# Pool's subtractions in pieces, a modulation sum spread ahead of the last feed-forward group, turned buffer places, and filler products in a router

## The chip, the cores and the metric

The kernel runs on one core of one Trainium2 chip. The metric is the device time of one execution in microseconds (us). Before the change three runs gave 2020.33 to 2025.81 us with a median of 2025.24 us. The engines of the core run side by side, each working through its own list of instructions in order: PE (matrix products; PEld is its weight load), DVE (VectorE), ACT (ScalarE), POOL (GpSimd) and SP, which here only starts the DMA loads of weights.

## The reference

The model is a backbone of two layers over 256 latent tokens and 256 context tokens of width 1024. Layer 0 runs grouped-query attention and gated linear attention side by side, then a dense SwiGLU with 3584 hidden features. Layer 1 is a neighbourhood attention and a top-2-of-8 mixture of experts with the same hidden width per expert. Each layer is modulated by six vectors of 1024 that come from the conditioning by one product with w_mod (adaln):

```python
for i in range(DEPTH):
    sh1, sc1, gt1, sh2, sc2, gt2 = _adaln(c, w_mod[i], b_mod[i])       # silu(c) @ w_mod + b_mod
    cmod = _adaln(c_ctx, w_mod[i], b_mod[i])
    h_lat = _modulate(_rmsnorm(x, g_norm1[i]), sh1, sc1)
    ...                                                               # mixer of layer i, y_lat, y_ctx
    x = x + gt1 * y_lat
    x = x + gt2 * ffn(_modulate(_rmsnorm(x, g_norm2[i]), sh2, sc2))    # SwiGLU in layer 0, experts in layer 1
    if need_ctx:
        ctx = ctx + cmod[2] * y_ctx
        ctx = ctx + cmod[5] * ffn(_modulate(_rmsnorm(ctx, g_norm2[i]), cmod[3], cmod[4]))
return _rmsnorm(x, g_final)

def _moe(h, w_router, wg, wu, wd):
    top_v, top_i = lax.top_k((h @ w_router).astype(jnp.float32), TOP_K)
    ...                                                               # softmax of the two, sum over experts
```

## The kernel before

Products of layer 0, of the neighbourhood attention's projections and of the dense feed-forward are done in three parts, because a weight and its input are each split into a high and a low half (hi and lo). For a weight of 1 MB (128 partitions x 2048 columns) `load_split` (L181 to L203) does that: SP loads it into a `raw` place, ACT casts it to `whi` (L201), and DVE subtracts the two into `wlo` (L202). Four of the weights, and the second pair of some projections, have POOL do this subtraction instead (`low = nc.gpsimd`). `raw`, `whi` and `wlo` each turn over a few places; a counter `state["n"]` decides which place the next `whi` and `wlo` get (three of each in the feed-forward). A place is free when its last reader is done.

A scheduler orders the instructions of each engine by priority in the order of the program; weight loads and their splits are moved ahead (`PREP`).

The parts that the change touches stand in the program in this order.

- **Layer 0's projections and output** (180 to 346 us): POOL subtracts `wlo8` (read by `pt_rb`) and `wlo12` (read by `po_gqa`).
- **The feed-forward of layer 0** (346 to 832 us): a loop over 7 groups of 512 hidden features. A group forms the products `pf_fg` and `pf_fu` for four blocks j, ACT and DVE form `sg` and `fT`, and then eight banks `fd{g}_{t}_{half}` of 12 products each go through DVE into the residual `xr` (`rtmp_ff`, then `xr`; L726, L727).
- **The modulation of layer 1**, three parts (1,0), (1,1), (1,2) of 2048 columns, is a sum on DVE (`adaln_sums`, L254 to L291) that is cut in 10 steps each: a load, eight products with a row block of `w_mod` (`acc`, L278 for the first and L280 for the others; (1,0) has three DVE instructions in each step instead of one), and an end with four products on PE and four transposes (`mod_ps`, `m_sb`, `modT_ps`, `mT`). `tick()` releases one step. The feed-forward loop calls it in two of a group's four blocks, and in all four blocks of the last group, so 16 of 30 steps; `tick(24)` (L971) releases the rest after the loop.
- **The norm after it** (`n3`): ACT squares, DVE `ms_n`, POOL `rs_n`, DVE `xc`, PE transposes `tf_n3`, and then per block of features ACT and DVE form `f_hi`, `tfraw` and `f_lo` (L369 to L372). Two streams of 256 tokens, context first. `mT` of part (1,0) and the parts after it go into this modulation. Then the projections `pt_vc` start, whose first weights are `whi`/`wlo` 56 and 57.
- **The neighbourhood attention's output** (to 1077 us): POOL subtracts the last such weight, read by `po_c`. POOL also adds a constant to `bias` (L1046).
- **The router** (1075 to 1094 us): for two blocks t of 128 tokens, `route_turn` transposes `xr` into `xT` (`rt`), `route_logits` squares and forms the norm and the logits (`lt_ps`, `lg_ps`, `lg`), `route_top` picks two experts (`sel`) and ranks tokens (`rk_ps`). Then PE gathers tokens (`gx`), and the first expert's products `pg_e` begin. From there to 2000 us the experts' products run.

Of the kernel before, what the change touches and what calls it, by code (L numbers as in the profile page):

```python
# [89 lines left out]
def kernel(ctx, tc, x, c, ctx_in, c_ctx, w_mod, b_mod, g_norm1, g_norm2, w_in_ab, g_q, g_k,  # L90
# [1034 lines left out]

    def route_turn(t):
        xt = xr[2 + t]
        for f4 in range(2):
            ps = bankB(f"rt_{t}_{f4}")
            for f in range(4):  # L1130
                o = (4 * f4 + f) * P
                nc.tensor.transpose(out=ps[:, f * P:(f + 1) * P], in_=xt[:, o:o + P], identity=ident)
            ins = (nc.scalar.copy if f4 or t == 0 else nc.vector.tensor_copy)(xT[:, t, 4 * f4:4 * f4 + 4, :],
                                                              ps.rearrange("p (f n) -> p f n", n=P))

        critical["turn"] = (ins.ins,)

    def route_logits(t):

        ssq = small.tile([P, 2], F32, tag="ssq2", name=f"ssq_n4_{t}")  # L1140
        ms = small.tile([P, 2], F32, tag="ms2", name=f"ms_n4_{t}")
        for h in range(2):
            hs = slice(h * 512, h * 512 + 512)
            nc.scalar.activation(xs_hi[t][:, hs], xr[2 + t][:, hs], AF.Square, accum_out=ssq[:, h:h + 1])
# [374 lines left out]
```

## Time and profile before

| what | value |
|---|---|
| median of 3 runs | 2025.24 us |
| the profiled execution's own time | 2025.02 us |
| its span (first to last instruction) | 2023.0 us |
| PE busy | 1933.7 us, 96% of the span |
| DVE busy | 750.6 us, 37% |
| ACT busy | 448.9 us, 22% |
| POOL busy | 148.9 us, 7% |
| DMA, moved | 493.32 MB |

The profiled execution lies 0.22 us below the median of the runs; 2.02 us of it are outside the span. In the pages below a time ahead of a row is counted from the start of the span. `PEclk` is the share of TensorE's full clock that was granted.

### The profile page before, as it was taken

The page shows a single profiled execution, that of the slowest core. Times are in us where ns is not written, and L with a number is a line of the kernel's source. Part 1 is how long each engine was busy: PE and PEld are TensorE (multiplying, and loading weights), DVE is VectorE, ACT ScalarE, POOL GpSimd, SP SyncE. Part 2 cuts the span into 40 slices and gives each one's busy share as a digit, 9 for nine tenths or more (in the row PEclk, how much of TensorE's full clock was granted, in tenths as well). Part 3 has the DMA queues.
Part 4 walks back from the last instruction along what each step waited for, and adds up shares of the span by engine and source line. Part 5 has one row for each costly group of instructions (what it writes and reads, how often), then busy time and mean ns, then how long its engine had stood idle before and what let it go on. Part 6 is the DMA issues. An engine that isn't in the chain of part 4 may idle for free.

```text
span 2023.0 us, 37020 instructions
## 1 busy us (share of the span) xinstructions
PE 1933.7 (96%) x16599; PEld 1182.6 (58%) x16599; DVE 750.6 (37%) x1185; ACT 448.9 (22%) x732; POOL 148.9 (7%) x145
## 2 busy tenths in 40 slices
PE   5999988999999999699998999999999999999996
PEld 3666666888888788467765354545444444544433
DVE  3246587656545555826773001111010101111022
ACT  4232255421222122235543001010100001010001
POOL 1102000000000000143211000000000100001010
PEclk8999999999999999799998999999999999999998
DMA  8624210433333334463336999999999999999991
GB/s 329 231 85 167 81 46 28 166 127 117 125 115 106 133 125 168 168 177 99 107 112 257 395 409 372 379 409 389 383 382 396 402 381 362 383 409 387 403 396 47
DMA packets 118901, 493.32 MB, mean 244 GB/s; under 512 B 10656, under 2 KB 50912, under 8 KB 98256
## 3 DMA queue, kind: packets, MB, share of 16 engines
q1 hardware_dynamic: 114096, 481.04, 62.4%
q0 software_dynamic: 3216, 7.03, 1.5%
q8 instruction: 132, 2.16, 0.4%
q10 hardware_dynamic: 1424, 2.81, 0.4%
q14 instruction: 33, 0.27, 0.0%
HBM read 486.13 MB, written 4.72 MB: 243 GB/s over the span
## 4 chain that ended last, share of the span: by engine, by line
PE 92%; DVE 4%; issue 1%; DMA 1%; ACT 1%; POOL 1%; ACTq 0%; SPq 0%; POOLq 0%; DVEq 0%
PE pu_e L1280 15%; PE pg_e L1280 14%; PE py_e L1280 14%; PE pf_fg L473 3%; PE pf_fg L471 3%; PE pf_fg L472 3%; PE fd L208 3%; PE pf_fu L473 3%; PE pf_fu L472 3%; PE pf_fu L471 3%; PE fd L206 3%; PE fd L207 3%; PE sc_e L1355 1%; PE mod_ps L245 1%; PE gx L1268 1%
## 5 line engine op out<-in xcount | busy, mean ns | idle before, releaser
L1280 PE MATMUL pu_e<-raw,X_all 128*32 128x448 f32 x3072 | 306.1, 540 | 0.0
L1280 PE MATMUL py_e<-raw,eT_e 128*32 128x256 f32 x5376 | 296.5, 379 | 0.0
L1280 PE MATMUL pg_e<-raw,X_all 128*32 128x448 f32 x3024 | 291.4, 539 | 0.0
L1280 PEld LDWEIGHTS py_e<-raw,eT_e 128*32 128x32 f32 x5376 | 190.5, 110 | 105.0 <-issue 5.4
L1280 PEld LDWEIGHTS pg_e<-raw,X_all 128*32 128x32 f32 x3024 | 100.0, 110 | 181.2 <-issue 175.5
L1280 PEld LDWEIGHTS pu_e<-raw,X_all 128*32 128x32 f32 x3072 | 98.5, 110 | 182.4 <-issue 178.4
L202 DVE TENSOR_TENSOR wlo<-raw,whi 128x2048 fp32r<-128x2048 f32 (+1 forms) x67 | 149.3, 2237 | 130.4 <-ACT whi L201 130.3
L201 ACT CAST whi<-raw 128x2048 fp32r<-128x2048 f32 (+1 forms) x73 | 134.9, 1859 | 257.8 <-PE fd L208 115.2
L1317 DVE TENSOR_TENSOR m_sb<-m_sb,pu_e 128x448 f32<-128x448 f32 x48 | 27.8, 604 | 393.6 <-PE pu_e L1280 393.6
L1313 ACT ACTIVATE m_sb<-pg_e 128x448 f32<-128x448 f32 x48 | 26.1, 544 | 512.8 <-PE pg_e L1280 512.8
L1358 POOL TENSOR_TENSOR xr<-xr,ytmp_e 128x512 f32<-128x512 f32 x28 | 35.2, 1280 | 822.5 <-DVE ytmp_e L1357 822.5
L473 PE MATMUL pf_fg<-f_hi,wlo 128*128 128x512 f32 (+1 forms) x240 | 92.5, 385 | 1.3 <-DVE ms_n L338 1.3
L472 PE MATMUL pf_fg<-f_lo,whi 128*128 128x512 f32 (+1 forms) x240 | 92.1, 384 | 0.0
L471 PE MATMUL pf_fg<-f_hi,whi 128*128 128x512 f32 (+1 forms) x240 | 92.0, 383 | 0.0
L471 PE MATMUL pf_fu<-f_hi,whi 128*128 128x512 f32 (+1 forms) x240 | 92.0, 383 | 0.0
L472 PE MATMUL pf_fu<-f_lo,whi 128*128 128x512 f32 (+1 forms) x240 | 91.6, 382 | 0.0
L473 PE MATMUL pf_fu<-f_hi,wlo 128*128 128x512 f32 (+1 forms) x240 | 91.2, 380 | 0.0
L208 PE MATMUL fd<-whi,fT 128*128 128x512 f32 x224 | 88.8, 396 | 0.0
L206 PE MATMUL fd<-whi,fT 128*128 128x512 f32 x224 | 88.5, 395 | 0.0
L207 PE MATMUL fd<-wlo,fT 128*128 128x512 f32 x224 | 88.3, 394 | 0.0
L1357 DVE SCALAR_TENSOR_TENSOR ytmp_e<-sc_e,comb,gate 128x512 f32<-128x512 f32 x32 | 23.6, 749 | 165.4 <-PE sc_e L1355 160.5
L1348 ACT COPY yF<-py_e 32x256 f32<-32x256 f32 x48 | 17.4, 362 | 265.9 <-PE py_e L1280 257.6
(373 smaller groups left out, 2707.8 us busy)
## 6 DMA issues: line engine op xcount, KB each, us to landing
raw<-in_w_moe_up_dram SPq DMA_DIRECT2D x128, 896.0 KB, 6.5
raw<-in_w_moe_down_dram SPq DMA_DIRECT2D x112, 1024.0 KB, 8.4
raw<-in_w_moe_gate_dram SPq DMA_DIRECT2D x126, 896.0 KB, 7.2
raw<-in_w_mod_dram SPq DMA_DIRECT2D x48, 1024.0 KB, 4.8
raw<-in_w_ff_gate_dram SPq DMA_DIRECT2D x14, 1024.0 KB, 4.9
raw<-in_w_ff_up_dram SPq DMA_DIRECT2D x14, 1024.0 KB, 4.9
raw<-in_w_ff_down_dram SPq DMA_DIRECT2D x14, 1024.0 KB, 4.9
raw<-in_w_in_c_dram SPq DMA_DIRECT2D x12, 1024.0 KB, 5.2
```

The source lines that it names most:

```text
L201: nc.scalar.copy(hi[:, c], raw[:, c])
L202: low.tensor_tensor(lo[:, c], raw[:, c], hi[:, c].bitcast(F32), op=ALU.subtract)
L206: nc.tensor.matmul(ps, ah, bh, start=start, stop=False)
L207: nc.tensor.matmul(ps, ah, bl, start=False, stop=False)
L208: nc.tensor.matmul(ps, al, bh, start=False, stop=stop)
L471: nc.tensor.matmul(ps, wh[:, k, ws], hh[:, k, ts], start=(k == 0), stop=False)
L472: nc.tensor.matmul(ps, wh[:, k, ws], hl[:, k, ts], start=False, stop=False)
L473: nc.tensor.matmul(ps, wl[:, k, ws], hh[:, k, ts], start=False, stop=(k == KT - 1))
L1280: nc.tensor.matmul(out[32 * q:32 * q + 32], lhsT, rhs[:, q], start=start, stop=stop, skip_group_check=True)
L1313: nc.scalar.activation(g, ps[s][:, 0:QW], AF.Silu)
L1317: nc.vector.tensor_tensor(gs[s], gs[s], ps[s][:, 0:QW], op=ALU.mult)
L1358: (nc.vector if self.last else nc.gpsimd).tensor_tensor(xr[2 + t][:, hs], xr[2 + t][:, hs], tmp, op=ALU.add)
```

## The change

Four things are done. First, where POOL subtracts in `load_split`, the subtraction is cut into instructions of 256 columns, so eight for a whole weight, and the addition to `bias` is cut in three. Second, `tick()` is called in all four blocks of each odd group and in two of an even group, so 20 steps of the modulation are released inside the feed-forward instead of 16, and `tick(24)` has 10 left. Third, the counter `state["n"]` is raised by one ahead of the feed-forward and once more ahead of the neighbourhood attention, so that each later weight takes the next place. The raised counter also changes the numbers in the names: `whi56` before is `whi58` after. Fourth, in the router the squares come ahead of the copies, POOL's `r_n4` with them, and 14 products `warm` that nobody reads are put between the steps on PE.

```diff
                 nc.scalar.copy(hi[:, c], raw[:, c])
-                low.tensor_tensor(lo[:, c], raw[:, c], hi[:, c].bitcast(F32), op=ALU.subtract)
+                if low is nc.vector:
+                    low.tensor_tensor(lo[:, c], raw[:, c], hi[:, c].bitcast(F32), op=ALU.subtract)
+                else:
+                    a, b, l = (w[:, c].rearrange("p k n -> p (k n)") for w in (raw, hi, lo))
+                    n = a.shape[-1]
+                    for o in range(0, n, 256):
+                        low.tensor_tensor(l[:, o:o + 256], a[:, o:o + 256], b[:, o:o + 256].bitcast(F32),
+                                          op=ALU.subtract)
...
+    state["n"] += 1
     queue_adaln((1, 0), (1, 1), (1, 2))
...
-                if j % 2 or g == NG - 1:
+                if j % 2 or g % 2:
                     tick()
...
+    state["n"] += 1
     for half in range(2):
         def ev_v(t, ps, half=half):
...
-        nc.gpsimd.tensor_tensor(bv, bv, cc(C_WIN, 64).unsqueeze(1).to_broadcast([P, 12, 64]), op=ALU.add)
+        for o in range(0, 12, 4):
+            nc.gpsimd.tensor_tensor(bv[:, o:o + 4], bv[:, o:o + 4],
+                                    cc(C_WIN, 64).unsqueeze(1).to_broadcast([P, 4, 64]), op=ALU.add)
...
+    warm_ps = bankA("warm")
+    def warm(n, after):
+        with tc.issue_after(after):
+            for _ in range(n):
+                nc.tensor.matmul(warm_ps[:, 0:256], ident, gate2[:, 0:256], start=True, stop=True)
+
     def route_turn(t):
...
+            sq = nc.scalar.activation(xs_hi[t][:, hs], xt[:, hs], AF.Square, accum_out=ssq[:, f4:f4 + 1]).ins
...
+            if t == 1:
+                warm(2 if f4 else 5, turned)
+            with tc.issue_after(sq):
+                (nc.scalar.copy if f4 or t == 0 else nc.vector.tensor_copy)(xT[:, t, 4 * f4:4 * f4 + 4, :],
+                                                                            ps.rearrange("p (f n) -> p f n", n=P))
...
+        if t == 1:
+            warm(3, mm.ins)
...
+        if t == 0:
+            warm(4, critical["rank"])
```

DVE at the end of the feed-forward, before: `fd6_2` and `fd6_3` are the last banks of the last group, `acc1_2` is the sum of part (1,2), `tfraw_n3` and `f_lo` the norm's stream of context tokens.

```order
L352 TENSOR_SCALAR xc1_5748<-xr2_1594,rs_n3_1_0_5753 128x1024
L727 TENSOR_TENSOR xr3_1595<-xr3_1595,rtmp_ff6_3_0_5600 128x512
L726 TENSOR_TENSOR rtmp_ff6_3_1_5616<-fd6_3_1_5603,gate0_0_5_2737 128x512
L727 TENSOR_TENSOR xr3_1595<-xr3_1595,rtmp_ff6_3_1_5616 128x512
L293 TENSOR_TENSOR m_sb1_1588<-mod_ps1_1_5626,m_sb1_1588 128x512
L278 TENSOR_SCALAR acc1_2_5639<-raw96_5640,cT_76 128x2048
L300 COPY mT1_96<-modT_ps1_1_5632 128x16 x2
L280 SCALAR_TENSOR_TENSOR acc1_2_5639<-raw97_5642,cT_76,acc1_2_5639 128x2048
L371 TENSOR_SCALAR tfraw_n3_0_0_5702<-tf_n3_0_0_5696,A3_1_5679,mT1_96 128x256
L280 SCALAR_TENSOR_TENSOR acc1_2_5639<-raw98_5645,cT_76,acc1_2_5639 128x2048
L372 TENSOR_TENSOR f_lo_2427<-tfraw_n3_0_0_5702,f_hi_828 128x256
L280 SCALAR_TENSOR_TENSOR acc1_2_5639<-raw99_5648,cT_76,acc1_2_5639 128x2048
```

The eight steps of `acc1_2` stand behind the last bank's residual, between the steps of the norm. After:

```order
L966 TENSOR_TENSOR sg6_3_5495<-sg6_3_5495,pf_fu6_1_1_5393 128x512
L301 TENSOR_TENSOR m_sb1_1595<-mod_ps1_1_5500,m_sb1_1595 128x512
L968 TENSOR_TENSOR fT1_6_5254<-sg6_3_5495,fT0_6_5253 128x512
L286 TENSOR_SCALAR acc1_2_5653<-raw96_5654,cT_76 128x2048
L308 COPY mT1_96<-modT_ps1_1_5506 128x16 x2
L288 SCALAR_TENSOR_TENSOR acc1_2_5653<-raw97_5656,cT_76,acc1_2_5653 128x2048
L734 TENSOR_TENSOR rtmp_ff6_0_0_5538<-fd6_0_0_5525,gate0_1_5_2744 128x512
L288 SCALAR_TENSOR_TENSOR acc1_2_5653<-raw98_5659,cT_76,acc1_2_5653 128x2048
L735 TENSOR_TENSOR xr0_1599<-xr0_1599,rtmp_ff6_0_0_5538 128x512
L288 SCALAR_TENSOR_TENSOR acc1_2_5653<-raw99_5662,cT_76,acc1_2_5653 128x2048
L734 TENSOR_TENSOR rtmp_ff6_0_1_5554<-fd6_0_1_5541,gate0_1_5_2744 128x512
L288 SCALAR_TENSOR_TENSOR acc1_2_5653<-raw100_5665,cT_76,acc1_2_5653 128x2048
```

The same sum now starts ahead of the first bank's residual (`fd6_0_0`) and stands between the residuals of the first four banks; its eighth step comes just before the residual of `fd6_1_1`, and the norm's `tfraw` and `f_lo` have none of it between them.

POOL in the same stretch, before: `rs_n3` are the norm's scales of four blocks of tokens, `rb_s` loads of a table, `wlo57` a subtraction for `pt_vc`.

```order
L340 TENSOR_TENSOR rs_n3_0_0_5686<-ms_n3_0_0_5684,mhalf_74 128x1
L340 TENSOR_TENSOR rs_n3_0_1_5693<-ms_n3_0_1_5691,mhalf_74 128x1
L340 TENSOR_TENSOR rs_n3_1_0_5753<-ms_n3_1_0_5751,mhalf_74 128x1
L340 TENSOR_TENSOR rs_n3_1_1_5760<-ms_n3_1_1_5758,mhalf_74 128x1
L987 MEMSET rb_s_5836 112x128
L989 DMA rb_s_5836<-in_rpb_c_dram 7x31 x3
L202 TENSOR_TENSOR wlo57_5878<-raw105_5875,whi57_5877 128x2048
L989 DMA rb_s_5836<-in_rpb_c_dram 7x31 x13
L990 DMA rb_d_5817<-rb_s_5836 7168x1x128
```

After:

```order
L997 MEMSET rb_s_5850 112x128
L999 DMA rb_s_5850<-in_rpb_c_dram 7x31 x6
L348 TENSOR_TENSOR rs_n3_0_0_5700<-ms_n3_0_0_5698,mhalf_74 128x1
L999 DMA rb_s_5850<-in_rpb_c_dram 7x31 x4
L348 TENSOR_TENSOR rs_n3_0_1_5707<-ms_n3_0_1_5705,mhalf_74 128x1
L999 DMA rb_s_5850<-in_rpb_c_dram 7x31 x6
L209 TENSOR_TENSOR wlo59_5892<-raw105_5889,whi59_5891 128x256 x8
L348 TENSOR_TENSOR rs_n3_1_0_5767<-ms_n3_1_0_5765,mhalf_74 128x1
L1000 DMA rb_d_5831<-rb_s_5850 7168x1x128
L348 TENSOR_TENSOR rs_n3_1_1_5774<-ms_n3_1_1_5772,mhalf_74 128x1
```

The subtraction (now `wlo59`, eight instructions) stands between the second and the third of the norm's scales, and the table's loads ahead of it; before, it stood behind all four.

PE in the router, before: `rt`, `lt_ps`, `lg_ps` and `rk_ps` are the router's steps, the last figure of a name the block t.

```order
L1152 MATMUL lt_ps0_7649<-xT_7616,wrA_6117 32x128 x8
L1132 MATMUL rt_1_1_7635<-ident_69,xr3_1595 128x128 x4
L1157 MATMUL lg_ps0_7660<-cst_71,lt0_7658 128x8
L1152 MATMUL lt_ps1_7673<-xT_7616,wrA_6117 32x128 x8
L1157 MATMUL lg_ps1_7684<-cst_71,lt1_7682 128x8
L1179 MATMUL rk_ps0_7705<-sel_7609,cst_71 128x8
L1178 MATMUL rk_ps1_7727<-sel_7609,cst_71 128x8
```

After:

```order
L1145 MATMUL warm_7675<-gate1_0_5_6129,ident_69 128x256 x5
L1158 MATMUL rt_1_1_7711<-ident_69,xr3_1602 128x128 x4
L1145 MATMUL warm_7675<-gate1_0_5_6129,ident_69 128x256 x2
L1175 MATMUL lt_ps0_7723<-xT_7674,wrA_6138 32x128 x8
L1180 MATMUL lg_ps0_7734<-cst_71,lt0_7732 128x8
L1175 MATMUL lt_ps1_7739<-xT_7674,wrA_6138 32x128 x8
L1180 MATMUL lg_ps1_7750<-cst_71,lt1_7748 128x8
L1145 MATMUL warm_7675<-gate1_0_5_6129,ident_69 128x256 x3
L1204 MATMUL rk_ps0_7774<-sel_7667,cst_71 128x8
L1145 MATMUL warm_7675<-gate1_0_5_6129,ident_69 128x256 x4
L1203 MATMUL rk_ps1_7800<-sel_7667,cst_71 128x8
L1204 MATMUL rk_ps1_7800<-sel_7667,cst_71 128x8
```

`lt_ps0` now stands behind the last transposes `rt_1_1`, and fillers stand ahead of them, behind them, ahead of `rk_ps0` and between the two rank products.

## Rows read from the trace of the kernel before

**Rows 1.** Windows: PE, PEld, DVE, ACT, POOL busy (instructions), PEclk, DMA share, GB/s.
```profile
400.00:450.00 50.00, 50.00 (x216) 40.14 (x215) 30.26 (x29) 11.71 (x11) 0.00 (x0) 1.00 0.35 121
1150.00:1200.00 50.00, 50.00 (x680) 24.89 (x676) 3.38 (x6) 0.36 (x1) 0.00 (x0) 1.00 1.01 410
```
**Rows 2.** SP's queue: line waited for, us in total, times, longest.
```profile
SPq L168 <- PE pu_e L1280: 263.6, 121, 5.9
```
**Rows 3.** Timeline of PE, end of the feed-forward: start, duration, operation, [idle before <-releaser].
```profile
831.57 0.40 PE L208 MATMUL fd<-whi,fT 128*128 128x512 f32 x1
...
839.20 1.12 PE L362 MATMUL tf_n<-ident,xc 128*128 128x128 f32 x4 [4.34 <-ACT tfraw_n L369]
847.11 0.47 PE L362 MATMUL tf_n<-ident,xc 128*128 128x128 f32 x1 [6.79 <-ACT tfraw_n L369]
853.60 1.94 PE L286 MATMUL mod_ps<-acc,one_of 128*32 128x512 f32 x8 [6.02 <-DVE acc L280]
...
864.15 0.66 PE L362 MATMUL tf_n<-ident,xc 128*128 128x128 f32 x4 [3.19 <-ACT tfraw_n L369]
...
875.29 0.40 PE L208 MATMUL pt_vc<-whi,f_lo 128*128 128x512 f32 x1
```
**Rows 4.** Timeline of DVE in the same stretch.
```profile
833.94 1.28 DVE L278 TENSOR_SCALAR acc<-raw,cT 128x2048 f32<-128x2048 f32 x1
...
858.28 4.31 DVE L372 TENSOR_TENSOR f_lo<-tfraw_n,f_hi 128x256 fp32r<-128x256 f32 x1
```
**Rows 5.** Windows in the same stretch.
```profile
801.00:831.00 30.00, 30.00 (x131) 24.23 (x130) 15.51 (x23) 6.47 (x9) 1.65 (x3) 1.00 0.10 36
855.00:860.00 5.00, 4.90 (x22) 3.56 (x19) 5.00 (x4) 2.78 (x3) 4.08 (x5) 0.64 0.32 74
```
**Rows 6.** Timeline of POOL in the same stretch.
```profile
857.72 4.58 POOL L202 TENSOR_TENSOR wlo<-raw,whi 128x2048 fp32r<-128x2048 f32 x1
```
**Rows 7.** POOL's groups: count, busy us, mean ns, idle before.
```profile
L202 POOL TENSOR_TENSOR wlo<-raw,whi 128x2048 fp32r<-128x2048 f32 x6 | 27.9, 4648 | 90.0 <-ACT whi L201 90.0
...
L1046 POOL TENSOR_TENSOR bias<-bias,cst 128x768 f32<-128x768 f32 x8 | 15.3, 1922 | 16.8 <-DMA bias<-rb_d 16.8
...
L1198 POOL TENSOR_TENSOR xs_lo<-scaled,xs_hi 128x512 fp32r<-128x512 f32 x4 | 5.0, 1282 | 13.8 <-ACT scaled L1197 13.8
```
**Rows 8.** Timeline of DVE beside POOL's subtractions.
```profile
275.66 4.51 DVE L727 TENSOR_TENSOR xr<-xr,rtmp_gla 128x512 f32<-128x512 f32 x1
...
1041.04 0.68 DVE L727 TENSOR_TENSOR xr<-xr,rtmp_c 128x512 f32<-128x512 f32 x1
...
1045.64 5.05 DVE L727 TENSOR_TENSOR xr<-xr,rtmp_c 128x512 f32<-128x512 f32 x1
```
**Rows 9.** Timeline of PE behind these.
```profile
187.60 0.79 PE L207 MATMUL pt_rb<-wlo,h_hi 128*128 128x512 f32 x1 [3.73 <-POOL wlo L202]
...
280.83 0.37 PE L798 MATMUL qT_ps<-ident_r,qhl 128*128 128x128 f32 x2 [4.19 <-DVE kT L788]
...
1051.68 0.65 PE L851 MATMUL o_c<-PT_c,vc 128*64 128x256 f32 x2 [2.20 <-DVE oC L854]
```
**Rows 10.** Timeline of PE where the feed-forward starts.
```profile
349.49 0.55 PE L362 MATMUL tf_n<-ident,xf 128*128 128x128 f32 x3 [2.99 <-DVE xf L352]
```
**Rows 11.** DVE's groups: the modulation's sums.
```profile
L280 DVE SCALAR_TENSOR_TENSOR acc<-raw,cT,acc 128x2048 f32<-128x2048 f32 x21 | 49.3, 2348 | 24.5 <-DMA raw<-in_w_mod_dram 24.4
...
L280 DVE SCALAR_TENSOR_TENSOR m_sb<-raw,cT,m_sb 128x1024 f32<-128x1024 f32 x7 | 9.0, 1279 | 0.0
```
**Rows 12.** Timeline of PE in the router.
```profile
1085.64 7.94 PE L1268 MATMUL gx<-m_sb,xr 128*128 128x192 f32 x32
1093.51 0.96 PE L1280 MATMUL pg_e<-first,X_all 128*32 128x448 f32 x8
```
**Rows 13.** Windows of `gx` alone: PE busy (instructions), PEclk.
```profile
1086.00:1088.00 2.00, 2.00 (x7) 2.00 (x7) 0.00 (x0) 0.50 0.99 412
1091.50:1093.40 1.90, 1.90 (x13) 1.79 (x11) 1.48 (x4) 1.00 1.03 426
```

More of the change, by code (lines that the diff above doesn't have):

```diff
@@ L1124, in rt @@
         return mop.tile([P, n], F32, name=name)
+    warm_ps = bankA("warm")
[3 more added lines that the diff above has]
+                nc.tensor.matmul(warm_ps[:, 0:256], ident, gate2[:, 0:256], start=True, stop=True)
     def route_turn(t):
         xt = xr[2 + t]
+        ssq = small.tile([P, 2], F32, tag="ssq2", name=f"ssq_n4_{t}")
+        ms = small.tile([P, 2], F32, tag="ms2", name=f"ms_n4_{t}")
         for f4 in range(2):
+            hs = slice(f4 * 512, f4 * 512 + 512)
+            sq = nc.scalar.activation(xs_hi[t][:, hs], xt[:, hs], AF.Square, accum_out=ssq[:, f4:f4 + 1]).ins
             ps = bankB(f"rt_{t}_{f4}")
@@ L1131, in route_turn @@
                 o = (4 * f4 + f) * P
[L1132 to L1144, printed above, removed]
+                turned = nc.tensor.transpose(out=ps[:, f * P:(f + 1) * P], in_=xt[:, o:o + P], identity=ident).ins
+            if t == 1:
[3 more added lines that the diff above has]
+                                                                            ps.rearrange("p (f n) -> p f n", n=P))
         nc.vector.tensor_scalar(ms[:, 0:1], ssq[:, 0:1], 1.0 / D, EPS, op0=ALU.mult, op1=ALU.add)
@@ L1148, in route_logits @@
         nc.gpsimd.tensor_tensor(r, ms[:, 1:2], mhalf[:, 0:1], op=ALU.pow)
+        scales.append(r)
+    def route_logits(t):
+        r = scales[t]
         lt_ps = bankB(f"lt_ps{t}", "y")
@@ L1156, in route_logits @@
         lg_ps = bankB(f"lg_ps{t}", "y")
-        nc.tensor.matmul(lg_ps[:, 0:NE], lt, cc(C_R, NE), start=True, stop=True)
+        mm = nc.tensor.matmul(lg_ps[:, 0:NE], lt, cc(C_R, NE), start=True, stop=True)
+        if t == 1:
+            warm(3, mm.ins)
         lg, eq = rt(f"lg{t}"), rt(f"eq{t}")
@@ L1187, in route_top @@
         tops.append(res)
-        scales.append(r)
     def route_rows():
```

## The prediction

> **What bounds the kernel now.** I read the windows first. In the feed-forward PE is busy in all 50 us of a 50 us window at full clock, with DVE at 30 of 50; in the experts it is busy in 50 of 50 too, with the DMA share at 1.01 [rows 1]. Which of the two sets the pace of the experts is told by the queue of SP: it waits 263.6 us for places that the `pu_e` products free [rows 2], so loads wait for PE. Whatever brings the first expert's product forward from 1093.51 [rows 12] therefore reaches the end in full, and what doesn't shorten a wait of PE ahead of that point is worth nothing. So the next view is PE's timeline, for the places where it idles. The largest is the end of the feed-forward: after the last `fd` product at 831.57 come waits of 4.34, 6.79, 6.02 and 3.19 us, 20.3 together, and the products of the first two blocks of tokens of `pt_vc` end only at 875.29 + 0.40 = 875.69 [rows 3]. Smaller ones follow a POOL subtraction: 3.73, 4.19 and 2.20 [rows 9], and 2.99 stands at the feed-forward's start [rows 10].
>
> **End of the feed-forward.** Before, DVE begins the sum of part (1,2) at 833.94 [rows 4], when PE has nothing left but what hangs on DVE, and PE gets on when the sum ends, at 853.60 [rows 3]. Eight steps are 1.28 [rows 4] and 7 x 2.35 [rows 11], 17.7 us. After, they stand among the residuals of the last group's eight banks. From 801 to 831 DVE has 15.5 us of work in 30 [rows 5], so about half of that stretch can take them. The eight banks hold 96 products; at 30 us for 131 [rows 5] that is 22.0 us for PE, and DVE's free part of it is about 22.0 x 0.48 = 10.6 us. DVE then has 17.7 us of sum and 2.3 us of a weight's subtraction to fit in, 20.0 against 10.6, so the last `fd` product comes 9.4 us later; I take 10, so 841.6. The raw loads of the sum are no hindrance, since the DMA engines move at a share of 0.10 there [rows 5].
>
> Behind it the weights for `pt_vc` are ready, since the turned place is free before the last bank and no longer after it. What is left on the path is the norm. POOL's `wlo59` now stands ahead of the third scale `rs_n3_1_0`. DVE's `xc1_0` waits for that scale, and the `f_lo` of the context stream are queued behind it. I expect POOL to start at about 843 and to hold them until about 849. Then `f_lo` and products overlap: 48 products by the same pace are 11.0 us, which makes the mark 859 to 861 instead of 875.69. That is 15 to 17 us. From it go 0 to 5 us for products at half clock: `fd` banks will now have gaps of 2 to 3 us between them as DVE frees them, and here the granted clock was 0.64 over 855 to 860, behind the long idle stretch [rows 5]. **I take 13**, with bounds of 5 (the last bank 15 us later instead of 10, and 5 at half clock) and 18 (DVE hides more, no half clock).
>
> **POOL's subtraction in pieces.** What one piece takes no row shows. From 512 to 768 columns POOL's instruction grows from 1.28 to 1.92 us [rows 7], 0.64 for 256 columns; the mean of the 2048-column one gives 4.65 / 8 = 0.58 as the lower bound. I take 0.7, with a fixed part, so 5.6 us for eight against 4.65 before. What the pieces give is elsewhere. While POOL subtracts, a DVE addition with two operands in SBUF takes 4.51 and 5.05 instead of 0.68 [rows 8], and `f_lo` 4.31 beside POOL's 4.58 [rows 4, 6]. If DVE gets in between two pieces, such a stall is at most one piece, so 4 us less. And PE needs no longer the whole subtraction: its waits in the new order are per row block, so after two pieces, 1.4 us, it can begin.
>
> - *`pt_rb` at 187.60.* PE waits 3.73 for POOL [rows 9]. It could begin about 3.2 us earlier, but then takes a row block of 1.4 us with every third product, which is no faster than three products of 0.79 with overlap [rows 9], so most is lost again: 0.5, bounds -3 (pieces delayed by DVE) and 3.
> - *Output of the linear attention, 280.83.* DVE's `xr` of 4.51 holds `kT`, for which PE waits 4.19 [rows 8, 9]: 3 of it goes, bounds 0 and 5 (with the half-clock products behind it).
> - *Output of the neighbourhood attention, 1051.68.* PE waits 2.20 and the 5.05 us `xr` is the reason [rows 8, 9]. Its products behind run at half clock for a while, so 4, bounds 0 and 6.
> - *`bias` in thirds.* No PE wait in this trace ends on it; 0, as the products cover it.
>
> The Trainium skill, in "SBUF — State Buffer", section "Who interferes with whom", says that a DVE instruction with two SBUF inputs and a GpSimd instruction that reads SBUF share a port pair, and that whoever starts first holds it for its whole instruction. The 5.05 against 0.68 agree with it. By that rule the lock ends with each piece, but it works both ways: POOL's pieces would also queue behind DVE's additions. What the rule leaves open is who is next when both wait, and no row here shows two POOL instructions back to back with DVE waiting.
>
> **Start of the feed-forward.** The turned place lets the second weight be cast earlier, ahead of the wait of 2.99 [rows 10], but pushes the `up` weight behind the second stream's norm steps. Fifteen products run earlier and stream 1 comes about 2 us later. I take -1 (a loss), bounds -4 and 2.
>
> **Ticks in the loop.** Odd groups now have four steps, even groups two. A step of (1,0) is 2.35 + 2 x 1.28 = 4.9 us [rows 11], others 2.35. A group lasts (831.57 - 349.49) / 7 = 69 us [rows 3, 10], and DVE has 20 of each 50 us free [rows 1]; four steps of (1,0) in group 1 instead of two add 9.8 us there. The free time covers it on average; a step between `sg` and `fT` delays PE only where the next bank isn't free. I take -0.5, bounds -3 and 0.
>
> **Router.** `gx` takes 7.94 us for 32 products [rows 12], seven in 2 us at a granted clock of 0.50 and thirteen in 1.9 us at 1.00 [rows 13]; at full clock 32 would take 4.7, so 3.2 less. The fillers (14 products) give PE work in the waits ahead of it. But the four between `rk_ps0` and `rk_ps1` stand on the path: by the column as `gx` at full clock (1.9 / 13 us for 192, so 0.2 for 256) they take 0.8 us, at half clock 1.6 [rows 13]. Against it the norm's scale no longer waits behind a copy, which I put at 0.5. I take 2, bounds -1 and 4.
>
> **Sum.** 13 + 0.5 + 3 + 4 - 1 - 0.5 + 2 = 21 us. From the profiled execution's 2025.02 (span 2023.0 and 2.02 outside it) this gives **2004 us**; the median of the runs is 0.22 higher, which I leave out. About 0.3%, 6 us, is what a measurement here can tell from no change, so faster ends at 2019 and slower begins at 2031.
>
> **Rivals.**
>
> 1. *DVE does not get between POOL's pieces* (0.15). POOL's next piece takes the ports again at once and a stall is 5.6 instead of 4.65. Then the 7.5 us at the three sites become about -2, and the end of the feed-forward loses 1 too: 21 - 10.5 = 10.5, so 2014 to 2015. For it: nothing in the trace shows a handover. Against it: a waiting instruction was there first.
> 2. *The stage of the last group takes back what its end gives* (0.14). DVE's sum delays the banks by the full 17.7 us instead of 10, fd products run at half clock, and the norm waits for POOL: 13 becomes 3, so 2014.
> 3. *Slower: steps four at a time make PE wait in groups 1, 3 and 5* (0.06). The place is the residuals and `fT` behind DVE's sums there. If nothing covers them, it costs four steps of 4.9 in group 1 and twice four of 2.35 in the others, 38.4 us, against 21.5 gained elsewhere: 2042. It decides from 27.5 us, so when 7 of 10 of these steps stand on the path. Against it speak the 27 us that DVE has free in a group by the windows [rows 1]; for it, that a step stands in front of what PE needs next.
> 4. *The places do not matter and the weights are late anyway* (0.05): the weights of `pt_vc` come by DMA later than the norm, and 13 becomes 9: 2008, in the likeliest's range.
>
> The likeliest holds 0.60; its own range is 1998 to 2010. The range for 8 in 10 reaches over rivals 1 and 2: **1995 to 2018**. Faster 0.82: the likeliest and rival 4 (0.65) and of rivals 1 and 2, each alone at 2014, a part of 0.17; the other 0.12 is where they come together (21 - 20.5, about 2024) or with losses in the smaller terms: same 0.12. Slower 0.06 is rival 3.
>
> **What would show it.** Right: DVE's last `acc` of (1,2) ends before the residual of `fd6_1_1`, the last `fd` product at 839 to 844, no wait of PE over 6 us between it and `pt_vc`, and the mark 14 to 17 us ahead of before. DVE's `xr` beside POOL's pieces at 1.5 us or less. `gx` at under 6 us. PE at 50 of 50 in the feed-forward's windows. Wrong: DVE instructions of 4 us or more beside pieces (rival 1), the last `fd` later than 847 (rival 2), waits of PE for `fT` or for a bank in groups 1, 3 and 5 (rival 3), or a first `gx` later than 1085.64 less the shift ahead of it.

## The result and the profile after

The changed kernel takes 2010.56 us in the median of four runs (2009.91 to 2011.83) against 2025.53 (2020.33 to 2025.91) before: a ratio of 0.9933, with a 95% interval of 0.9916 to 0.995. The forecast was 2004 with a range of 1995 to 2018. So the sign and the range held, and of 21 us forecast 15 came. The profiled execution's span went from 2023.0 to 2007.9 us.

Where the 15 us come from is read best by stages. Each stage below runs from one mark on PE's timeline to the next, so that a shift is counted once, where it arises. A stage that an edit doesn't touch differs by up to 0.8 us between most single traces, and by up to 1.8 between some (the stage of `fd` is +9.5 to +11.3 in kernels that differ from the changed one elsewhere).

| stage on PE, from the mark before to | before, us | after | difference | forecast |
|---|---|---|---|---|
| last `pt_rb` (from its first) | 54.68 | 56.62 | +1.94 | -0.5 |
| last `po_gqa` | 108.35 | 103.63 | -4.72 | -3 |
| last `pf_fu` | 463.16 | 464.64 | +1.48 | +1.5 |
| last `fd` | 22.31 | 33.40 | +11.09 | +10 |
| 48th product of `pt_vc` (the forecast's mark) | 43.72 | 21.71 | -22.01 | -23 |
| last `pt_vc` | 39.41 | 43.17 | +3.76 | 0 |
| first `po_c` | 111.30 | 111.80 | +0.50 | 0 |
| last `po_c` | 48.65 | 43.56 | -5.09 | -4 |
| first `gx` | 10.59 | 10.87 | +0.28 | -2, both |
| first expert product | 7.87 | 5.44 | -2.43 | |

With 0.05 at the start this makes -15.15, and the experts behind it take as long as before.

PE at the end of the feed-forward, where [rows 3] had waits of 4.34, 6.79, 6.02 and 3.19 us (start, duration, operation, idle before it and what ended that):

```profile
826.49 0.50 PE L214 MATMUL fd<-whi,fT 128*128 128x512 f32 x1 [2.64 <-DVE rtmp_ff L734]
...
834.42 0.60 PE L214 MATMUL fd<-whi,fT 128*128 128x512 f32 x1 [1.65 <-DVE rtmp_ff L734]
...
849.78 0.80 PE L216 MATMUL pt_vc<-whi,f_lo 128*128 128x512 f32 x1 [4.23 <-DVE f_lo L380]
...
866.32 0.66 PE L370 MATMUL tf_n<-ident,xc 128*128 128x128 f32 x4 [1.82 <-ACT tfraw_n L377]
...
870.61 0.50 PE L214 MATMUL pt_vc<-whi,f_hi 128*128 128x512 f32 x1 [1.92 <-ACT vc L1020]
...
884.26 0.50 PE L215 MATMUL pt_vc<-wlo,f_hi 128*128 128x512 f32 x1 [1.96 <-DVE wlo L203]
...
906.52 1.88 PE L339 MATMUL gate_ps<-m_sb,ident 128*128 128x512 f32 x4
```

The 20.3 us are gone, as forecast, and `fd` banks now wait for DVE (2.64, 1.65). What is new are 4.23 us for one `f_lo`, 1.82 for the second stream's norm, 1.96 for a subtraction by DVE, and gate products (906.52) that before filled a gap and now stand behind `pt_vc`. Before, that gap looked like this:

```profile
875.53 2.74 PE L331 MATMUL gate_ps<-m_sb,ident 128*128 128x512 f32 x6
878.94 1.12 PE L331 MATMUL gate_ps<-m_sb,ident 128*128 128x512 f32 x2 [0.67 <-ACT gate L332]
881.23 0.50 PE L206 MATMUL pt_vc<-whi,f_hi 128*128 128x512 f32 x1 [1.16 <-ACT vc L1009]
```

The 0.67 and 1.16 are all the waits of the stage to the last `pt_vc` before, 1.83 us. Now they are 1.82, 1.92 and 1.96, together 5.70, and the difference is the +3.76 of the table to 0.1. The gate products behind it (1.88) account for +1.72 up to the first `pf_cq`, the products that follow. DVE in the same stretch:

```profile
810.68 1.28 DVE L286 TENSOR_SCALAR acc<-raw,cT 128x2048 f32<-128x2048 f32 x1
...
829.21 2.35 DVE L288 SCALAR_TENSOR_TENSOR acc<-raw,cT,acc 128x2048 f32<-128x2048 f32 x1
...
833.68 0.68 DVE L734 TENSOR_TENSOR rtmp_ff<-fd,gate 128x512 f32<-128x512 f32 x1
...
844.36 5.03 DVE L735 TENSOR_TENSOR xr<-xr,rtmp_ff 128x512 f32<-128x512 f32 x1
849.32 0.41 DVE L380 TENSOR_TENSOR f_lo<-tfraw_n,f_hi 128x256 fp32r<-128x256 f32 x1
849.85 0.75 DVE L360 TENSOR_SCALAR xc<-xr,rs_n 128x1024 f32<-128x1024 f32 x1
...
878.46 5.75 DVE L203 TENSOR_TENSOR wlo<-raw,whi 128x2048 fp32r<-128x2048 f32 x1 [7.91 <-ACT whi L201]
```

The sum of part (1,2) runs from 810.68 to 831.5, ahead of the residual of `fd6_1_1` (833.68). Then an `xr` takes 5.03 us, and `f_lo` stands behind it, ahead of the `xc` that needs the third scale. POOL explains both long rows:

```profile
839.91 3.41 POOL L999 DMA_DIRECT2D rb_s<-in_rpb_c_dram  x6
843.34 5.50 POOL L209 TENSOR_TENSOR wlo<-raw,whi 128x256 fp32r<-128x256 f32 x8
848.81 1.01 POOL L348 TENSOR_TENSOR rs_n<-ms_n,mhalf 128x1 f32<-128x1 f32 x1
...
869.96 7.87 POOL L1055 DMA_DIRECT2D bias<-rb_d  x12 [15.20 <-DMA rb_d<-rb_s]
877.84 10.39 POOL L1058 TENSOR_TENSOR bias<-bias,cst 128x256 f32<-128x256 f32 x9
```

The eight pieces of `wlo59` run from 843.34 to 848.84 with nothing between them (8 x 0.69), and `xr` comes out at 849.39; the bias thirds hold DVE's subtraction for 5.75 us in the same way. In both cases DMA issues of POOL (L999, L1055) stand right ahead. At two other places DVE did get in: these rows of its timeline answer to [rows 8], where the `xr` took 4.51 and 5.05.

```profile
277.59 0.73 DVE L735 TENSOR_TENSOR xr<-xr,rtmp_gla 128x512 f32<-128x512 f32 x1
...
1037.69 1.23 DVE L735 TENSOR_TENSOR xr<-xr,rtmp_c 128x512 f32<-128x512 f32 x1
```

The granted clock, for [rows 5] (busy PE, PEld, DVE, ACT, POOL with instructions, PEclk, DMA share, GB/s):

```profile
825.00:830.00 5.00, 3.51 (x11) 2.80 (x12) 5.00 (x5) 1.87 (x1) 0.00 (x0) 0.78 1.02 375
...
835.00:840.00 5.00, 5.00 (x17) 3.98 (x16) 3.36 (x7) 1.15 (x2) 4.97 (x10) 0.69 0.63 207
850.00:855.00 5.00, 5.00 (x14) 4.02 (x15) 4.37 (x12) 3.65 (x9) 4.46 (x4) 0.50 0.98 297
```

Between the waits for `fd` banks the products run at half clock for some of the time (0.78 and 0.69), and for all of the window behind the 4.23 us wait (0.50). In the router ([rows 12]) `gx` takes 5.50 instead of 7.94:

```profile
1070.75 1.97 PE L1145 MATMUL warm<-gate,ident 128*128 128x256 f32 x8
...
1072.92 5.50 PE L1294 MATMUL gx<-m_sb,xr 128*128 128x192 f32 x32
1078.36 0.96 PE L1306 MATMUL pg_e<-first,X_all 128*32 128x448 f32 x8
```

### The profile page after: what moved, and what is told of

The parts are those of the page before. It is cut to its first block, busy times and chain, and to the rows that moved or that the text cites. A ratio compares the mean times of both kernels' runs of the same rounds, so it can differ in the third digit from the quotient of the medians.

```text
span 2007.9 us, 37143 instructions
## 1 busy us (share of the span) xinstructions
PE 1934.4 (96%) x16627; PEld 1180.6 (59%) x16627; DVE 744.7 (37%) x1185; ACT 448.1 (22%) x732; POOL 170.6 (8%) x203
## 3 DMA queue, kind: packets, MB, share of 16 engines
HBM read 486.13 MB, written 4.72 MB: 244 GB/s over the span
## 4 chain that ended last, share of the span: by engine, by line
PE 91%; DVE 3%; ACT 2%; issue 2%; DMA 1%; POOL 1%; ACTq 0%; SPq 0%; POOLq 0%; DVEq 0%
PE pu_e L1306 15%; PE pg_e L1306 14%; PE py_e L1306 14%; PE pf_fu L479 3%; PE pf_fu L480 3%; PE pf_fu L481 3%; PE pf_fg L479 3%; PE pf_fg L480 3%; PE pf_fg L481 3%; PE fd L216 2%; PE fd L215 2%; PE fd L214 2%; PE sc_e L1381 1%; PE mod_ps L253 1%; PE o_c L859 1%
```

## Experiments

The theory: pieces let DVE in where nothing prevents it, and gain there; the end of the feed-forward gained less than forecast because POOL and DVE stand in each other's way there; the fillers raise the clock of `gx`. Each ratio stands beside runs of the kernel before on the same chip. Their medians were 2024.43 for the three parts alone; 2024.88 for `rb_s` on ACT's queue, `wlo59` on DVE, the first subtraction whole and bias whole; 2024.27 for the counter-test, the places back, no fillers and the three edits combined; and 2023.72 for the last run. The intervals of the ratios overlap for most of the kernels that differ by under 4 us from the changed one, so their comparison rests on the stages.

**The parts alone**, each on the kernel before. Pieces:

```diff
+                    for o in range(0, n, 256):
+                        low.tensor_tensor(l[:, o:o + 256], a[:, o:o + 256], b[:, o:o + 256].bitcast(F32),
...
+        for o in range(0, 12, 4):
+            nc.gpsimd.tensor_tensor(bv[:, o:o + 4], bv[:, o:o + 4],
```

> The kernel before with the first part of the change alone: POOL's subtractions of a weight in pieces of 256 columns and the addition to bias in thirds. Theory (additive, as the stage marks of the two traces say): the output of layer 0's projection to pt_rb loses 2.0 us, since DVE's instructions go between the pieces and the subtraction lasts about 9.3 us; the linear attention's output gains 4.6, the neighbourhood attention's output gains 5.1, the rest is 0: 2025.5 - 7.7 = about 2018, and the xr beside the pieces at the output of the neighbourhood attention takes under 1.5 us. Rival (POOL keeps the ports between its pieces): each stall is 5.6 us instead of 4.65, time 2027, that xr over 5 us.

Measured: 2016.84 us, ratio 0.9958 (0.9941 to 0.9975). By stages +1.66 to the last `pt_rb`, -4.70 to `po_gqa`, -5.09 in the stage of `po_c`. The handover happens; and it gives 1.2 us between `pf_cq` and `po_c`, where I had counted 0. It didn't happen at the end of the feed-forward: beside the pieces that follow the loads of `rb_s` there, an `f_lo` took 5.26 us (0.41 alone), and the stages to the 48th and to the last product of `pt_vc` are +0.98 and +1.52.

Feed-forward:

```diff
+    state["n"] += 1
     queue_adaln((1, 0), (1, 1), (1, 2))
...
-                if j % 2 or g == NG - 1:
+                if j % 2 or g % 2:
...
+    state["n"] += 1
     for half in range(2):
```

> The kernel before with the second and third part alone: 20 steps of the modulation inside the feed-forward and the places turned; POOL subtracts in one instruction, the router as before. Theory: the feed-forward's start loses 1.5 us, its end gains 8 to 10 up to the last product of pt_vc (in the changed kernel 7.2, less a wait of 2.0 that pieces of the bias addition cause there): 2025.5 + 1.5 - 9 = about 2018. Rival (the end's gain needs the pieces, because the whole subtraction of 4.6 us ahead of the third norm scale holds DVE as long as eight pieces of 5.5 do, or longer): 2020 to 2023.

Measured: 2019.01 us, ratio 0.9971 (0.9958 to 0.9983). By stages +1.07 to the last `pf_fu`, then +11.60, -23.91 and +3.11 up to the last `pt_vc`, -9.2 in all. So the end's gain doesn't need the pieces; with them it is 7.2, two less. The +3.11, and the +1.72 up to the first `pf_cq`, stand here without any piece.

Router:

```diff
+            sq = nc.scalar.activation(xs_hi[t][:, hs], xt[:, hs], AF.Square, accum_out=ssq[:, f4:f4 + 1]).ins
...
+                warm(2 if f4 else 5, turned)
...
+            warm(3, mm.ins)
...
+            warm(4, critical["rank"])
```

> The kernel before with the fourth part alone: squares first and 14 filler products in the router. Theory: gx takes 5.5 us instead of 7.9 at full clock, and that is all: 2025.5 - 2.2 = about 2023. Rival (the fillers delay the second ranking as much as the clock gives back): 2025 to 2026, first gx over 1 us later.

Measured: 2022.87 us, ratio 0.9991 (0.9981 to 1.0). By the time alone that can't be told from no change, but the stages of the router give +0.28 and -2.44. The three parts make -6.2 and -7.2 over the whole span and -2.2 in the router's two stages, 15.6 together for the 15.15 of the whole change; the rest of the router's run, where nothing was changed, is another -1.2. By the medians it is 7.6, 5.4 and 1.6, 14.6 for 15.0. So they add, as far as the scatter lets one tell.

**POOL's DMA issues ahead of the pieces.**

```diff
-        nc.gpsimd.dma_start(rb_s[7 * h:7 * h + 7, 48:79], rpb_c[0, h, 4:11, :])
+        nc.scalar.dma_start(rb_s[7 * h:7 * h + 7, 48:79], rpb_c[0, h, 4:11, :])
```

> The changed kernel with one thing different: the 16 loads of the table rb_s are issued from ACT's queue instead of POOL's, so that no DMA issue of POOL stands ahead of wlo59's pieces. In the changed kernel an xr beside these pieces took 5.03 us, while beside the pieces at two other places it took 1.2 and 0.7. Theory one (POOL's DMA issues just ahead are why DVE does not get between those pieces): xr falls under 1.5 us, PE's wait of 4.2 for f_lo shrinks to about 1, and the time falls by 3 to 4 us to about 2007. Theory two (it has nothing to do with the issues; who gets the ports between two pieces is settled by something else): xr beside the pieces stays at 4 us or more and the time stays within 1.5 us of 2010.6, or falls only by what the earlier start of the norm's scales gives.

Measured: 2006.46 us, ratio 0.9911 (0.9894 to 0.9927). DVE beside the pieces (timeline):

```profile
843.68 0.68 DVE L735 TENSOR_TENSOR xr<-xr,rtmp_ff 128x512 f32<-128x512 f32 x1
...
848.91 0.75 DVE L360 TENSOR_SCALAR xc<-xr,rs_n 128x1024 f32<-128x1024 f32 x1 [4.10 <-POOL rs_n L348]
```

POOL in the same stretch:

```profile
841.87 6.50 POOL L209 TENSOR_TENSOR wlo<-raw,whi 128x256 fp32r<-128x256 f32 x8 [4.70 <-ACT whi L201]
848.33 0.55 POOL L348 TENSOR_TENSOR rs_n<-ms_n,mhalf 128x1 f32<-128x1 f32 x1
```

The `xr` takes 0.68, and the pieces 6.50 instead of 5.50, so DVE went between them. But the wait only moved: `xc` now waits 4.10 us for the third scale behind the pieces, `f_lo` stands behind it, and PE waits longer for it than before:

```profile
850.05 0.80 PE L216 MATMUL pt_vc<-whi,f_lo 128*128 128x512 f32 x1 [5.23 <-DVE f_lo L380]
```

The 48th product isn't earlier (-8.0 for both stages against -10.9). What is gained comes from behind it: the stages to the last `pt_vc` and to the first `pf_cq` are 0.0 and 0.0 instead of +3.76 and +1.72. The bias table is late and its thirds are out of the way, and the gate products fill the gap as before. The time was right and the way to it wrong.

The counter-test puts issues where there were none:

```diff
                 nc.scalar.copy(hi[:, c], raw[:, c])
+                if state["c"] == 71:
+                    idle = dram.tile([6, P, 16], F32, name="idle")
+                    for h in range(6):
+                        nc.gpsimd.dma_start(idle[h], hi[:, 0, 0:16].bitcast(F32))
```

> The changed kernel with six DMAs (128 x 16 each, from whi73 to a DRAM buffer that nobody reads) issued by POOL right ahead of the pieces of wlo73, the subtraction for the neighbourhood attention's output, where DVE got in between the pieces in each run so far. Theory one (POOL's DMA issues right ahead keep DVE out of the gaps): a DVE instruction that shares the ports, xr or the pr_c scaling, takes 3 us or more beside these pieces. Theory two (the issues have nothing to do with it): none over 1.5 us. The pieces themselves come about 3 us later in both, which may cost up to 3 us.

Measured: 2012.69 us (two runs), ratio 0.9943 (0.9923 to 0.9963). POOL's timeline, with the issues and the pieces:

```profile
1037.48 3.25 POOL L205 DMA_DIRECT2D idle<-whi  x6 [32.89 <-ACT oC L865]
1040.75 5.72 POOL L213 TENSOR_TENSOR wlo<-raw,whi 128x256 fp32r<-128x256 f32 x8
```

DVE beside them:

```profile
1042.02 3.87 DVE L843 TENSOR_SCALAR pr_c<-pr_c,rsm_c 128x512 f32<-128x512 f32 x1
```

The same scaling in the changed kernel, first beside pieces of an earlier subtraction and then beside these, with no issue ahead of either:

```profile
926.50 0.92 DVE L839 TENSOR_SCALAR pr_c<-pr_c,rsm_c 128x512 f32<-128x512 f32 x1
...
1042.62 0.64 DVE L839 TENSOR_SCALAR pr_c<-pr_c,rsm_c 128x512 f32<-128x512 f32 x1
```

The scaling of `pr_c` takes 3.87 us beside pieces that follow DMA issues, and 0.92 and 0.64 beside these without them; alone it takes 0.47. So theory one holds in kind, but not without exception. Six of the kernels run here have `wlo59` in pieces behind such issues and an `xr` beside them: it took 5.03, 4.59, 5.63, 5.05, 2.73 and, with bias whole, 0.68, where it started just as the first piece ended. The nine bias thirds behind issues held a subtraction by DVE for 3.62 to 5.75 us in five kernels, and let it in at the end of the running piece in two (2.38 and 2.44; alone it takes 2.28). Where no issue stood ahead, DVE was never held for more than one piece. In what way the issues keep DVE out, and what lets it in after all, these runs don't tell.

**`wlo59` on DVE.**

```diff
-    ON_POOL = (8, 12, 57, 71)
+    ON_POOL = (8, 12, 71)
```

> The changed kernel with the subtraction wlo59 done by DVE (2.3 us, one instruction) instead of by POOL's eight pieces. Theory (the pieces ahead of the third norm scale and the 5 us xr beside them are what was lost against the forecast at the end of the feed-forward): the wait of 4.2 us for f_lo goes, DVE pays 2.3 us in a stretch where it is the pacing engine: gain 1 to 4 us, 2007 to 2009. Rival (DVE paces this stretch, so 2.3 us more on it cost 2.3 us): 2010 to 2013.

Measured: 2007.15 us, ratio 0.9911 (0.9894 to 0.9927). The two stages to the 48th product make -15.4 instead of -10.9, so the pieces had cost 4.5 us there. Behind the mark +3.51 and +1.72 stay, so the pieces of `wlo59` are not what cost there. The rest of the stages is as in the changed kernel to 0.9 us, but 1.5 us longer in the router, where the fillers ran at half clock, as the window of the fillers says (PEclk is the third number from the end):

```profile
1065.00:1070.00 5.00, 5.00 (x18) 4.23 (x19) 3.13 (x21) 0.00 (x0) 0.00 (x0) 0.66 1.02 429
```

**The first subtraction whole.**

```diff
-                    for o in range(0, n, 256):
+                    step = n if state["c"] == 8 else 256
+                    for o in range(0, n, step):
```

> The changed kernel with the first POOL subtraction (wlo8, read by pt_rb) in one instruction again, the others in pieces. Theory (pieces interleave with DVE's additions there, so the last pieces come late and PE waits four times, 5.3 us together, instead of once, 3.7): 2.0 us faster, 2008.5. Rival (the loss at that place is an accident of the clock and not of the pieces): within 0.5 us of 2010.6.

Measured: 2009.16 us, ratio 0.9923 (0.9906 to 0.9939). The time lies between theory and rival; the place itself speaks for the theory: the stage of `pt_rb` is +0.02, with one wait of 3.73 again. In the changed kernel it was +1.94, with these four waits of PE:

```profile
184.45 0.50 PE L215 MATMUL pt_rb<-wlo,h_hi 128*128 128x512 f32 x1 [0.53 <-POOL wlo L209]
...
186.33 0.51 PE L215 MATMUL pt_rb<-wlo,h_hi 128*128 128x512 f32 x1 [0.91 <-POOL wlo L209]
...
188.86 0.50 PE L215 MATMUL pt_rb<-wlo,h_hi 128*128 128x512 f32 x1 [1.56 <-POOL wlo L209]
...
192.28 0.80 PE L215 MATMUL pt_rb<-wlo,h_hi 128*128 128x512 f32 x1 [2.34 <-POOL wlo L209]
```

and this subtraction on POOL:

```profile
182.91 9.31 POOL L209 TENSOR_TENSOR wlo<-raw,whi 128x256 fp32r<-128x256 f32 x8 [1.48 <-ACT whi L201]
```

Eight pieces last 9.31 us instead of 4.68, because DVE's instructions go between.

**Bias whole.**

```diff
-        for o in range(0, 12, 4):
-            nc.gpsimd.tensor_tensor(bv[:, o:o + 4], ..., op=ALU.add)
+        nc.gpsimd.tensor_tensor(bv, bv, cc(C_WIN, 64).unsqueeze(1).to_broadcast([P, 12, 64]), op=ALU.add)
```

> The changed kernel with the addition to bias in one instruction of 768 columns again. Theory (nine thirds in a row held DVE's subtraction for a projection for 5.75 us, and PE waited 2.0 for it): whole additions hold it no longer than the thirds, 3 times 1.9 is 5.7 us, so no change within 1 us at that place, 2010 to 2011; the thirds are worth nothing. Rival (with the thirds DVE gets in at least between different bias tables, with whole ones it does not, or the other way round): a change of 1 to 3 us.

Measured: 2011.94 us (2008.98 to 2013.57), ratio 0.9933 (0.9916 to 0.9949): the thirds are worth nothing that can be told. But the reason in the theory failed: beside the whole additions the subtraction by DVE takes 2.62 us instead of 5.75, and PE's wait of 1.96 for it is gone, so the rival's other way round is what happened at that place. The stage to the last `pt_vc` is +3.11 here and +3.76 with thirds; products that ran at half clock took most of the 1.96 back, where the changed kernel had a clock of 1.00 throughout this stage (PEclk is again third from the end):

```profile
875.00:880.00 5.00, 5.00 (x16) 3.98 (x15) 0.00 (x0) 0.00 (x0) 5.00 (x8) 0.67 0.60 150
```

**The places back.**

```diff
-    state["n"] += 1
     queue_adaln((1, 0), (1, 1), (1, 2))
...
-    state["n"] += 1
     for half in range(2):
```

> The changed kernel without the two raised counters, so with the places as before. Theory (the turned place lets the first weight of pt_vc be cast and subtracted ahead of the last fd bank): the first pt_vc product comes 3 to 6 us later, the feed-forward's start gets its 1.5 us back, so 2012 to 2015. Rival (the places don't matter, the norm comes later than the weight anyway): only the 1.5 us at the start, 2009.

Measured: 2005.0 us, ratio 0.9906 (0.9889 to 0.9923), 5.6 us faster than the change. Both theories fall short. The first 1.85 us are at the feed-forward's start, as both had it (-0.37 instead of +1.48). At the end, the two stages to the 48th product make -10.1 against -10.9: the weight does come later, but what it costs is 0.9, not 3 to 6, and that is within the scatter of a stage. And behind it the stages are 0.00 and 0.00 instead of +3.76 and, up to the first `pf_cq`, +1.72, and on PE the gate products lie in the gap again:

```profile
861.90 2.74 PE L339 MATMUL gate_ps<-m_sb,ident 128*128 128x512 f32 x6
865.31 1.12 PE L339 MATMUL gate_ps<-m_sb,ident 128*128 128x512 f32 x2 [0.67 <-ACT gate L340]
867.60 0.50 PE L214 MATMUL pt_vc<-whi,f_hi 128*128 128x512 f32 x1 [1.16 <-ACT vc L1018]
```

This gap is as before the change. The router is 1.5 us longer, with the fillers at half clock. What cost behind the mark I read as the order into which the scheduler put the rest when the first weight got ready earlier; that order by itself was not tried. The turned places alone don't make the loss: with `rb_s` on ACT's queue they stay turned, and the two stages are 0.0 as well.

**No fillers.**

```diff
-            for _ in range(n):
+            for _ in range(0):
```

> The changed kernel without the 14 filler products, squares still first. Theory (the fillers keep the clock up for gx): gx takes 7.9 us again and the first expert product comes about 2.4 us later, less what the four fillers between the rank products cost: 2012 to 2013. Rival (the squares' order did it, the fillers only cost): 2009 to 2010.

Measured: 2012.38 us, ratio 0.9943 (0.9927 to 0.996).

```profile
1071.05 0.60 PE L1204 MATMUL rk_ps<-sel,cst 128*128 128x8 f32 x2 [1.63 <-DVE sel L1200]
1071.50 8.03 PE L1294 MATMUL gx<-m_sb,xr 128*128 128x192 f32 x32
1079.46 4.72 PE L1306 MATMUL pg_e<-first,X_all 128*32 128x448 f32 x48
```

`gx` takes 8.03 again. The first `gx` comes 1.0 us sooner without fillers (-0.72 against +0.28) and they give 2.5 back: the gain is theirs; what squares first gives, 0.7, is no more than untouched stages vary.

**Combined.** The first subtraction whole, `wlo59` on DVE and `rb_s` on ACT's queue:

> The changed kernel with three edits at once: the first POOL subtraction whole again, wlo59 on DVE, and the loads of rb_s on ACT's queue. Alone they gave 1.4, 3.4 and 4.1 us. Theory (they mend different waits: one at pt_rb, one ahead of the third norm scale, one behind the bias table, which comes later then): most of the sum, 2002 to 2004. Rival (the last two mend the same wait): 2005 to 2006.

Measured: 1998.57 us (1998.35 to 1999.57), ratio 0.9875 (0.9859 to 0.9892), the fastest of all, 12 us below the change. PE's waits there:

```profile
824.05 0.57 PE L215 MATMUL fd<-whi,fT 128*128 128x512 f32 x1 [2.62 <-DVE rtmp_ff L735]
...
831.98 0.51 PE L215 MATMUL fd<-whi,fT 128*128 128x512 f32 x1 [1.65 <-DVE rtmp_ff L735]
...
841.93 0.66 PE L371 MATMUL tf_n<-ident,xc 128*128 128x128 f32 x4 [0.79 <-DVE rtmp_ff L735]
843.58 0.73 PE L217 MATMUL pt_vc<-whi,f_lo 128*128 128x512 f32 x2 [0.99 <-DVE f_lo L381]
```

None is over 2.7, and the two stages to the 48th product make -14.5, those behind it 0. The three gave 1.4, 3.4 and 4.1 alone and 12 together, more than their sum of 8.9. By stages each edit does at its own place about what it did alone: `pt_rb` +0.03 (alone +0.02), the end of the feed-forward -14.5 (-15.4 with `wlo59` on DVE alone), 0 behind the mark (0 with `rb_s` on ACT's queue alone). What two of them lost elsewhere when alone doesn't come back: 2.9 us at the end of the feed-forward, where with `rb_s` on ACT's queue the third scale still waited for pieces, and 1.5 in the router with `wlo59` on DVE, where the fillers ran at half clock.

The same with the places as before:

> The three edits combined (first POOL subtraction whole, wlo59 on DVE, loads of rb_s on ACT's queue) and the places as before too. Theory (what the turned places cost at the feed-forward's start, 1.85 us by the stage marks, is apart from what the three edits mend; at its end the order of the gate products that the places spoilt is already mended by the three): 1998.6 - 1.8 = about 1997. Rival (the places' cost at the end adds as well): 1993 to 1995. Other rival (with wlo59 on DVE the old place of the first pt_vc weight, free only after a late fd bank, is late again): 1999 to 2001.

Measured: 2003.0 us (2000.29 to 2003.8), ratio 0.9898 (0.9881 to 0.9915), nearest to the other rival and above it too. The stage of the last `pf_fu` gives 2.1 us back, but the two to the 48th product are -11.1 instead of -14.5:

```profile
838.44 4.48 DVE L203 TENSOR_TENSOR wlo<-raw,whi 128x2048 fp32r<-128x2048 f32 x2
842.85 0.68 DVE L735 TENSOR_TENSOR rtmp_ff<-fd,gate 128x512 f32<-128x512 f32 x1
```

Both weights are now subtracted in a row behind the last `fd` bank, and the last residual waits for them. In the combined kernel the first of them stands at 829.04, between the banks. The router's stage is 1.5 us longer, the fillers being at half clock, and 1.5 more lie ahead of the first `pt_rb`, where nothing was changed. So of the 4.4 us between the two medians the places account for 1.3: 3.4 that the turned place is worth at the feed-forward's end here, less 2.1 that it costs at its start. By the same count it costs 6.5 in the changed kernel (1.85 at the start and 5.5 behind the mark, less 0.9), so its value hangs on what else DVE and POOL do in that stretch.

## Why the prediction was right, and where it was not

- *What bounds the kernel* held: all that came forward ahead of 1093.51 came out at the end, 15.15 us by stages and 15.1 in the span.
- *The last `fd`* was forecast 10 us later and came 11.09 later by its stage; DVE's sum by its durations against PE's banks gave it, and the half clock of some banks, which the forecast had put behind them, is in the rest. That it ended at 841.81 where 841.6 was forecast is partly luck: the stages ahead of it came 1.25 us sooner, which the forecast of that moment leaves out.
- *The mark* was forecast at 859 to 861, and up to 5 us later for half clock, and came at 863.52; by the two stages the gain is 10.9 where I took 13. POOL's `wlo59` did hold the norm from 843.34 to 849.8, as forecast (843 to 849), but the way there was another, and the agreement is luck. I had `f_lo` behind an `xc` that waits for the scale. In fact `f_lo` (849.32) stood ahead of that `xc` (849.85), behind the `xr` that the pieces held. With `rb_s` on ACT's queue that `xr` was free, and then the wait for the scale came as I had it, with 5.23 us of PE. The products behind the 4.23 us wait ran at half clock, which is the rest.
- *Behind the mark* is the step that failed: I let the forecast end at the 48th product and took all behind it as unchanged. There 5.5 us went back: 3.76 to the last `pt_vc`, by longer waits for the second stream's norm (1.82), for ACT's `vc` (1.92) and for DVE's subtraction beside the bias thirds (1.96), and 1.72 to the first `pf_cq`, by gate products that no longer lay in a gap. So the term of 13 was 10.9 less 5.5. The loss needs the turned places and POOL's issues of `rb_s` together, since it is 0 when either goes. The 1.2 us gained in the stage behind are the pieces' own (-1.22 with the pieces alone, -0.02 with the feed-forward's part alone).
- *Pieces* gained 4.7 and 5.1 where I took 3 and 4. At `pt_rb` they cost 1.9 where I took a gain of 0.5; my bound named the reason (pieces delayed by DVE), and the subtraction's 9.31 us show it. The eight pieces alone took 5.50 us where I took 5.6.
- *Rival 1* came true at one of four places, `wlo59`'s. I had made one rule of it, that DVE gets in or does not. The runs show both, and holding over several pieces occurred only where POOL's DMA issues stood right ahead.
- The rule of the Trainium skill ("SBUF — State Buffer", "Who interferes with whom"), that the port pair is held for one whole instruction, fits the 1.23 and 0.73; the 5.03 us beside eight separate instructions goes beyond it.
- *Ticks*: PE was busy in 50 of 50 us in each window from 400 to 800; rival 3 did not occur. *Start*: together with the ticks a loss of 1.48 where I took 1.5, but the split was wrong, so the match is luck: the places cost 1.85 where I took 1, and the ticks nothing (-0.37 with the places back) where I took 0.5. *Router*: 2.15 gained for 2, with sizes that cancel: `gx` gained 2.44 where I took 3.2, as it takes 5.50 us at a clock of 1.00 and not 4.7. The four fillers on the path took 1.97 us at a clock of 1.00 and not 0.8, since I counted a filler as one record of the trace and the 14 are 28 there; but without fillers the first `gx` came only 1.0 sooner.
- *Rival 4* was too tame: the places did matter, to the bad, by 5.6 us.
- *The signs* named: the last `fd`, the longest wait of PE behind it, `gx` and the feed-forward's windows came as said. The `xr` beside `wlo59` (5.03) and the mark, 12.2 us ahead of before and not 14 to 17, did not.

## What to carry to other kernels

When a long stall goes, follow the order behind the point where the forecast ends until two timelines run in parallel again; here 5.5 of 13 us were lost behind the mark. Cutting one engine's instruction into pieces helps those that wait for the ports and hurts those that wait for the whole, so cut it only where the first are on the path. And an edit that helps in one order may cost in another: by the stages that it touches, the turned place cost 6.5 us in the changed kernel and was worth 1.3 with the three other edits.

## What was not expected of the hardware

- DVE took turns with POOL's pieces wherever no DMA issue of POOL stood right ahead: an `xr` of 0.70 to 0.73 at the linear attention's output and of 1.22 to 1.23 at the neighbourhood attention's, in each kernel that has them. Behind such issues an `xr` was held over several pieces, up to 5.63 us, in five kernels of six, an `f_lo` for 5.26 in a seventh, and the scaling for 3.87 in the counter-test. What lets it in at other times is open.
- A piece of 256 columns takes 0.71 to 0.74 us at a pitch of 0.69, so eight take 5.50 alone, and up to 9.31 with DVE between them.
- Fillers kept the clock at 1.00 through the router in most traces; in three of them (`wlo59` on DVE, the places back, the last kernel) they ran at half clock themselves and cost 1.5 us more, and `gx` took 5.50 us at 1.00 even so.
